# A one-core decoder layer: cached rows are compressed before the first projection instead of beside the state space

## The chip, the cores and the metric

The kernel runs on one core of one Trainium2 chip. The metric is the device time of one execution in microseconds (us), as the median of several runs; lower is better. The profile is of one execution on the same kind of core.

## What is computed

One layer of a decoder, for 512 new tokens of a prompt and for 8 samples of one token each (520 columns in all), in fp32. A conditioning vector gives shift, scale and gate (`mod`) for a normalised input; one projection `w_in` gives the input `u` of a state space model, queries, three pairs of keys and values, and gates. The state space model and an attention with three branches run on their parts; both go through an output projection and then an MLP.

```python
mod = silu(c) @ w_ada + b_ada                     # conditioning, in blocks of 512 columns
h = rmsnorm(x, norm_attn) * (1 + sc1) + sh1
u, q, k_c, v_c, k_s, v_s, k_w, v_w, g = split(h @ w_in)
# state space: B of lambda, u -> scan over time -> C, then
z = gelu(y + d * u);  o_ssm = z * sigmoid(z @ ssm_w_glu)
# compressed branch: cached rows (8 samples x 1024 rows) and new rows
h_first  = einsum('bcjgd,jdh->bcgh', chunks, w1[:16])
h_second = einsum('bcjgd,jdh->bcgh', chunks, w1[16:])
k_cmp = einsum('bngh,hd->bngd', gelu(h_first[:, :-1] + h_second[:, 1:] + pe_term), w2)
```

The change concerns the compressed branch of the samples (the cached rows of each sample, 1 MB, are gathered, turned so that the feature dimension lies on partitions, multiplied by `w1`, put through GELU and multiplied by `w2`), and when this is done.

## The kernel before

Matmuls of projections and MLP are made of three products of rounded halves (wH·xH, wL·xH, wH·xL). The program is written stage by stage; a scheduler then orders the instructions of each engine, so rows of one stage stand among rows of others. Instructions marked `keep_in_program_order` stay in the order in which they are written. Buffers are tiles of named pools: a tile can be written when what read its predecessor in the same place is done, and a pool's memory passes to the next pool when the pool is closed.

The stages, in the order of the program:

- **Constants and loads.** `load_cache(b)` (L246) gathers the 1 MB of sample b on the POOL queue. `late` (L279) issues small loads there.
- **The state space's lambda tables** (L407 to L544), mostly on VectorE: exponentials, sines, tables `tab`, `lr`, `li`.
- **Cache compression, two samples at a time** (bp = 0 to 3). `turned(bp)` (L353) makes 32 transposes of 128x128 on TensorE (`pxc`, L368) into eight PSUM tiles of tag `tr`, which has two buffers, and copies these into two tiles `xc`, one for keys and one for values: four copies a tile, of 64x256, on VectorE (L377) and ScalarE (L375) in turn for bp 0 and 1, all on ScalarE for bp 2 and 3. `compressed(bp)` (L380) multiplies `xc` by `w1` into `ph` (L387: 64 matmuls of some 128 columns for bp 0, 32 of 256 columns for the others), applies GELU (`hidden`, L305) and multiplies by `w2` (`pk`, L396 and L398). An fp32 matmul of this kind is two instructions in the trace.
- **Conditioning** `ada(s)` (L319): 2 MB of `w_ada` in two or four loads (L330), 8 matmuls `pada` (L334), a copy `mrow`, 4 transposes `padt` (L339). s = 0 to 3 are needed before the u projection.
- **u projection** (`pj`, L605), then the first key and value projection `kv_proj(0)` (`pkv`, L647).
- **State space loop** (L727 to L822): 8 groups `qd`. Each makes `BP` and `Cb` (L752 to L759, VectorE), `pm0` and its transposes (L766, L767), sends M to HBM and reads it back as `Tz` (L772, L774, SP queue), makes `pvs` (L792), turns, scans and turns back (`W`, `Rr`, `Sx`, L799 to L811, with ScalarE copies `Vp` and `Rp`), and multiplies `Tz` and `Cb` into `pys` (L819, L820), which goes to HBM as `yscr` (L822). Among the groups stand compressions 2 and 3 with their transposes, `ada` 5 to 9 and `compress_prompt` (L691), which compresses the prompt's own rows with the same `w1`.
- **kv_proj(1), kv_proj(2), q projection** (`pj` again, L900 to L916), whose outputs go to a pool `outs` that takes memory freed by the loop. `state_space_outputs(q)` (L884), for q = 0 to 3, reads `yscr` back as `yc` (L888, one buffer), makes `yf` (L890) and a GELU into `zf`, which is the memory of `uT`.
- **Attention**, among it the scores `psc` (L1159) and `pst` (L1217 to L1219), window rows `rwin`, sums `poS`, and the gate matmuls `pg` (L1273) of the state space, which need all four parts of `zf`; then **out projection** and **MLP** (L1401).

## Time and profile before

| | before |
|---|---|
| median of 3 runs | 896.86 us (896.5 to 897.89) |
| the profiled execution | 896.29 us |
| its span in the trace | 894.6 us |
| TensorE busy (PE) | 844.3 us, 94% |
| VectorE (DVE), ScalarE (ACT), GpSimd (POOL) busy | 525.0, 388.2, 65.2 us |

The span is the time from the first to the last instruction of the trace. Busy times of an engine are sums over its instructions; neighbouring TensorE rows overlap a little. A line such as "L387 PE" is line 387 of the kernel before.

### The profile page before, as it was taken

How to read it: one execution, taken by the hardware profiler on the slowest of the kernel's cores; microseconds unless marked ns; L12 is line 12 of the kernel's file. 1: busy time of each engine (PE TensorE's matmuls, PEld its weight loads, DVE VectorE, ACT ScalarE, POOL GpSimd, SP SyncE). 2: the span in 40 equal slices, each digit the busy share in tenths (PEclk: the TensorE clock that was granted, in tenths of full speed). 3: DMA queues.
4: the chain of work that ended last, by engine and by line, in shares of the span. 5: the costliest groups of instructions: out<-in, count | busy, mean ns of one | idle time of the engine just before them, and what ended most of it. 6: DMA issues, size and time to landing. Idle time of an engine off the chain costs nothing.

```text
span 894.6 us, 16415 instructions
## 1 busy us (share of the span) xinstructions
PE 844.3 (94%) x6517; PEld 747.3 (84%) x6517; DVE 525.0 (59%) x1413; ACT 388.2 (43%) x880; POOL 65.2 (7%) x147
## 2 busy tenths in 40 slices
PE   3799998999999899999889999999999999999995
PEld 2567897788998676756579999999999999999995
DVE  6676656759747975667578964443233444434534
ACT  2545326634435656546655554441111344433422
POOL 6001201000134200100000000000000000000000
PEclk9999999999999999999999999999999999999998
DMA  8956678366456620303257552333333333332202
GB/s 294 318 193 217 194 169 239 123 204 194 127 179 206 203 95 1 142 1 142 78 206 227 161 189 85 95 95 95 95 95 95 95 95 95 96 88 70 79 1 95
DMA packets 111836, 122.36 MB, mean 137 GB/s; under 512 B 24500, under 2 KB 91880, under 8 KB 109584
## 3 DMA queue, kind: packets, MB, share of 16 engines
q1 hardware_dynamic: 102256, 89.71, 33.0%
q0 software_dynamic: 5488, 29.99, 9.8%
q10 hardware_dynamic: 4016, 1.62, 0.7%
q8 instruction: 51, 0.84, 0.4%
q14 instruction: 25, 0.20, 0.1%
HBM read 112.47 MB, written 13.03 MB: 140 GB/s over the span
## 4 chain that ended last, share of the span: by engine, by line
PE 86%; DMA 6%; ACT 3%; DVE 2%; issue 1%; SPq 0%; ACTq 0%; DVEq 0%
PE pdn L1401 21%; PE pup L1401 20%; PE pj L605 5%; PE pwo L1401 5%; PE pkv L647 5%; PE ph L387 5%; DMA wada<-w_ada 5%; PE pada L334 2%; PE ptp L1246 2%; PE po L1253 2%; PE pS L1032 2%; PE pg L1273 2%; PE pst L1217 2%; PE pys L819 2%; PE pkT L1023 1%; PE pst L1218 1%
## 5 line engine op out<-in xcount | busy, mean ns | idle before, releaser
L1401 PE MATMUL pdn<-hidL,wH 128*128 128x256 f32 (+1 forms) x480 | 136.1, 284 | 0.0
L1401 PE MATMUL pdn<-hidH,wL 128*128 128x256 f32 (+1 forms) x480 | 135.9, 283 | 0.0
L1401 PE MATMUL pdn<-hidH,wH 128*128 128x256 f32 (+1 forms) x480 | 135.4, 282 | 0.0
L1401 PE MATMUL pup<-h2L,wH 128*128 128x256 f32 (+1 forms) x480 | 135.0, 282 | 0.0
L1401 PE MATMUL pup<-h2H,wL 128*128 128x256 f32 (+1 forms) x480 | 135.0, 282 | 0.0
L1401 PE MATMUL pup<-h2H,wH 128*128 128x256 f32 (+1 forms) x480 | 134.1, 283 | 0.0
L1401 PEld LDWEIGHTS pup<-h2L,wH 128*128 128x128 f32 x480 | 90.4, 188 | 0.8 <-DVE rs_t L97 0.8
L1401 PEld LDWEIGHTS pdn<-hidH,wL 128*128 128x128 f32 x480 | 90.6, 189 | 0.0
L1401 PEld LDWEIGHTS pdn<-hidL,wH 128*128 128x128 f32 x480 | 90.4, 188 | 0.1
L1401 PEld LDWEIGHTS pup<-h2H,wL 128*128 128x128 f32 x480 | 90.4, 188 | 0.0
L1401 PEld LDWEIGHTS pdn<-hidH,wH 128*128 128x128 f32 x480 | 90.4, 188 | 0.0
L1401 PEld LDWEIGHTS pup<-h2H,wH 128*128 128x128 f32 x480 | 89.6, 188 | 0.0
L63 ACT CAST wH<-wdn 128x1024 fp32r<-128x1024 f32 x30 | 31.5, 1050 | 114.0 <-PE pdn L1401 104.1
L64 DVE TENSOR_TENSOR wL<-wup,wH 128x1024 fp32r<-128x1024 f32 x30 | 36.7, 1224 | 58.1 <-ACT wH L63 58.1
L64 DVE TENSOR_TENSOR wL<-wdn,wH 128x1024 fp32r<-128x1024 f32 x30 | 36.8, 1225 | 54.2 <-ACT wH L63 54.2
L387 PE MATMUL ph<-xc,w 128*128 128x256 f32 (+2 forms) x320 | 65.4, 356 | 1.2 <-DVE xc L377 0.7
L387 PEld LDWEIGHTS ph<-xc,w 128*128 128x128 f32 x320 | 52.8, 203 | 12.9 <-issue 6.4
L63 ACT CAST wH<-wup 128x1024 fp32r<-128x1024 f32 x30 | 31.5, 1050 | 48.0 <-PE pup L1401 37.6
L1479 ACT ACTIVATE rl<-pup 128x256 f32<-128x256 f32 (+1 forms) x64 | 24.4, 384 | 48.9 <-PE pup L1401 48.8
L375 ACT COPY xc<-pxc 64x256 f32<-64x256 f32 x96 | 32.1, 366 | 20.8 <-DVE xc L377 18.2
L1410 DVE SCALAR_TENSOR_TENSOR xT<-pdn,mod,xT 128x256 f32<-128x256 f32 x32 | 15.2, 479 | 43.2 <-PE pdn L1401 43.2
L1480 DVE TENSOR_TENSOR rl<-rl 128x256 f32<-128x256 f32 (+1 forms) x64 | 27.1, 425 | 22.6 <-ACT rl L1479 22.6
(557 smaller groups left out, 2023.9 us busy)
## 6 DMA issues: line engine op xcount, KB each, us to landing
wada<-w_ada SPq DMA_DIRECT2D x20, 1024.0 KB
wup<-w_up SPq DMA_DIRECT2D x16, 1024.0 KB
wdn<-w_down SPq DMA_DIRECT2D x16, 1024.0 KB
wo<-w_out SPq DMA_DIRECT2D x8, 1024.0 KB
wada<-w_ada SPq DMA_DIRECT2D x8, 512.0 KB
rwin<-state_win SPq DMA_DIRECT2D x4, 1024.0 KB
new_win_sample<-state_win POOLq DMA_DIRECT2D x2, 2044.0 KB, 8.9
wkv<-w_in SPq DMA_DIRECT2D x3, 1024.0 KB
```

The source lines that it names most:

```text
L63: nc.scalar.copy(h, src)
L64: nc.vector.tensor_tensor(l, src, h, ALU.subtract)
L334: nc.tensor.matmul(ps[k % 4 * 32 : k % 4 * 32 + 32], cT[:, k], rs[k // kp][:, k % kp], start=(k < 4), stop=(k >= 4))
L375: nc.scalar.copy(dst[:, :, :, hf], srcv[:, :, :, hf])
L387: nc.tensor.matmul(phv[:, lo:hi, 0:w], w1[n][:, r_], xc[n][:, lo:hi, r_ % 8, off : off + w], start=(r_ == 0), stop=(r_ == 15))
L605: nc.tensor.matmul(ps[:, 0:HB], w[:, k], x[:, k, hc], start=(k == 0 and n == 0), stop=(k == KT - 1 and n == 2))
L647: nc.tensor.matmul(ps[0:mp, 0:nw], x[:, k, tok], w[:, k % 4], start=(k == 0 and n == 0), stop=(k == KT - 1 and n == 2))
L819: nc.tensor.matmul(py[:, c], Tz[:, :, :, g].rearrange("p t c -> p (t c)"), U[:, qd * GQ + g], start=True, stop=False)
L1032: nc.tensor.matmul(S[b4 * 32 : b4 * 32 + 32], q4[:, 4 * grp + b4], kts[b4], start=True, stop=True)
L1401: nc.tensor.matmul(ps[:, 0 : b - a], w, x[:, a:b], start=first and n == 0, stop=last and n == 2)
L1479: nc.scalar.activation(rl, ps[:, 0 : b - a], AF.Relu)
L1480: nc.vector.tensor_tensor(rl, rl, rl, ALU.mult)
```

## The change

The compressions of all four sample pairs, and `ada` 0 to 3, are written before the u projection, in the order compressed(0), ada(0), turned(1), compressed(1), ada(1), turned(2), compressed(2), ada(2), turned(3), ada(3), the x transposes, compressed(3). The first conditioning matmul of ada(0) to ada(3) stays in that written order, and ada(1) loads in four parts. The four copies of a PSUM tile in `turned` become two of 64x512, one on VectorE and one on ScalarE, for all bp. The pool with `w1` and `xc` is closed before the u projection and its memory goes to `outs`; `compress_prompt` loads `w1` again (two loads of 1 MB on SP). In the state space loop stand kv_proj(1) after group 0, `compress_prompt` after group 1, kv_proj(2) after group 3, and `ada` 5 to 9 after groups 1, 2, 4, 5 and 6. The q projection has its output memory from the beginning. `state_space_outputs` still takes its memory when the loop's pool is closed.

```diff
@@ loads
     load_cache(2)
-    xr = []
-    for h in range(2):
-        r = p0.tile([P, 2, D], F32, tag="xr%d" % h, name="xr")
...
+    load_cache(3)
...
@@ ada
-    def ada(s, tag, parts=2):
+    def ada(s, tag, parts=2, pin=False):
...
         for k in range(KT):
-            nc.tensor.matmul(ps[k % 4 * 32 : k % 4 * 32 + 32], cT[:, k], rs[k // kp][:, k % kp], start=(k < 4), stop=(k >= 4))
+            mm = nc.tensor.matmul(ps[k % 4 * 32 : k % 4 * 32 + 32], cT[:, k], rs[k // kp][:, k % kp], start=(k < 4), stop=(k >= 4))
+            if pin and k == 0:
+                tc.keep_in_program_order(mm)
@@ turned
-                        for hf in range(2):
-                            if (g + hf) % 2 or bp > 1:
-                                nc.scalar.copy(dst[:, :, :, hf], srcv[:, :, :, hf])
-                            else:
-                                nc.vector.tensor_copy(dst[:, :, :, hf], srcv[:, :, :, hf])
+                        if g:
+                            nc.scalar.copy(dst, srcv)
+                        else:
+                            nc.vector.tensor_copy(dst, srcv)
@@ before the u projection
-    load_cache(3)
-    ada(0, "ad", 4)
-    ada(1, "ad")
+    def two_caches(bp):
+        for b in (2 * bp, 2 * bp + 1):
+            load_cache(b)
+        xcs[bp] = turned(bp)
+
     compressed(0, xcs.pop(0))
-    ada(2, "ad", 4)
+    ada(0, "ad", 4, True)
     xcs[1] = turned(1)
-    ada(3, "ad")
+    compressed(1, xcs.pop(1))
+    ada(1, "ad", 4, True)
+    two_caches(2)
+    compressed(2, xcs.pop(2))
+    ada(2, "ad", 4, True)
+    two_caches(3)
+    ada(3, "ad", 2, True)
...
+    compressed(3, xcs.pop(3))
     p0x.close()
-    compressed(1, xcs.pop(1))
+    cpx.close()
...
+    left = ExitStack()
+    outs = left.enter_context(tc.tile_pool(name="outs", bufs=1, reuse_waits="tile"))
+    QS = outs.tile([P, NH, T], F32R, name="QS")
...
@@ compress_prompt
         for n in range(2):
+            w = rawt("w1p").rearrange("p (r h) -> p r h", r=16)
+            load_w1(n, w)
...
@@ state space loop
-        if qd in (0, 3):
-            b = 4 + 2 * (qd // 3)
-            load_cache(b)
-            load_cache(b + 1)
-            xcs[b // 2] = turned(b // 2)
-        if qd in (2, 5):
-            compressed(2 + qd // 3, xcs.pop(2 + qd // 3))
-        if qd in (1, 3, 4, 6, 7):
-            ada((5, 6, 7, 8, 9)[(1, 3, 4, 6, 7).index(qd)], "ad")
-        if qd == 6:
-            compress_prompt()
...
+        if qd in (0, 3):
+            kv_proj(1 + qd // 3)
+        if qd == 1:
+            compress_prompt()
...
+        if qd in (1, 2, 4, 5, 6):
+            ada((5, 6, 7, 8, 9)[(1, 2, 4, 5, 6).index(qd)], "ad")
@@ behind the loop
-    for c in (1, 2):
-        kv_proj(c)
-        state_space_outputs((c - 1,))
+    state_space_outputs((0,))
     for s in range(2):
...
-        state_space_outputs((2 + s,))
+        state_space_outputs((1,) if s == 0 else (2, 3))
```

The scheduler's order shows what this moves. On TensorE, during compressed(0) (`ph`; w_155 holds the key weights and w_156 the value weights), before:

```order
L334 MATMUL pada<-wada,cT 32x512 x2
L387 MATMUL ph<-xc,w_155 128x128 x3
L334 MATMUL pada<-wada,cT 32x512 x2
L387 MATMUL ph<-xc,w_155 128x128 x6
L435 MATMUL pss<-ones,xsq 8x1 x8
L387 MATMUL ph<-xc,w_155 128x128 x3
L387 MATMUL ph<-xc,w_156 128x130 x3
L334 MATMUL pada<-wada,cT 32x512 x2
L387 MATMUL ph<-xc,w_156 128x130 x13
L339 MATMUL padt<-ident,mrow 128x128 x4
L387 MATMUL ph<-xc,w_156 128x128 x14
L334 MATMUL pada<-wada,cT 32x512
```

and now, the rows that do the same work:

```order
L431 MATMUL pxs<-ident,xsr 128x64
L389 MATMUL ph<-xc,w_155 128x130
L389 MATMUL ph<-xc,w_155 128x128 x15
L437 MATMUL pss<-ones,xsq 8x1 x8
L389 MATMUL ph<-xc,w_155 128x128
L389 MATMUL ph<-xc,w_156 128x130 x16
L389 MATMUL ph<-xc,w_156 128x128 x16
L532 MATMUL pct<-ident,crw 128x128 x4
L538 MATMUL pst_479<-ident,srw 128x128 x2
L557 MATMUL pvec<-ident,vrow 128x84
L371 MATMUL pxc<-ident,rc 128x128 x4
L398 MATMUL pk<-hg,w2k 64x128 x2
```

The conditioning matmuls `pada` that stood between the `ph` rows are gone from there; they come after the transposes `pxc` of turned(1) have begun. Those transposes now follow in one run, with `pada` of ada(0) among them and no `ph`.

On TensorE at the end of the state space loop, before, between the first `pys` matmul of the last group and its others (`psf` are transposes of the final state):

```order
L682 MATMUL pkt<-ident,kvt 128x128 x2
L647 MATMUL pkv<-wH,hH 128x280
L647 MATMUL pkv<-wL,hH 128x280
L647 MATMUL pkv<-wH,hL 128x280
L827 MATMUL psf<-ident,SF 32x128
L647 MATMUL pkv<-wH,hH 128x280
L647 MATMUL pkv<-wL,hH 128x280
L647 MATMUL pkv<-wH,hL 128x280
L647 MATMUL pkv<-wH,hH 128x280
```

and now, from the last `pys` of the seventh group to the first `pys` of the eighth:

```order
L828 MATMUL pys<-Sx,Cb 128x80
L1220 MATMUL pst<-KH,QS 128x512
L1221 MATMUL pst<-KL,QS 128x512
L1222 MATMUL pst<-cmaskr,identr 128x128
L800 MATMUL pvs<-U,Bb 128x72 x4
L1220 MATMUL pst<-KH,QS 128x128
L1221 MATMUL pst<-KL,QS 128x128
L1222 MATMUL pst<-cmaskr,identr 128x128
L1220 MATMUL pst<-KH,QS 128x384
L1221 MATMUL pst<-KL,QS 128x384
L1222 MATMUL pst<-cmaskr,identr 128x128
L827 MATMUL pys<-U,Tz 128x80
```

Rows of key and value projection stood around the last group before; now `pst`, of attention, stands there, and the rows of the q projection are all ahead.

On SP's queue behind the loop, before:

```order
L822 DMA yscr<-ys 128x320
L1263 DMA wglu<-ssm_w_glu 128x4x512
L822 DMA yscr<-ys 128x320
L888 DMA yc<-yscr 16x8x80 x4
L1150 DMA rwin<-state_win 128x2x1024 x3
L888 DMA yc<-yscr 16x8x80 x12
L1150 DMA rwin<-state_win 128x2x1024
```

and now:

```order
L830 DMA yscr<-ys 128x320
L780 DMA mscr<-M_2804 128x64
L782 DMA Tz<-mscr 128x8x64
L830 DMA yscr<-ys 128x320 x2
L893 DMA yc<-yscr 16x8x80 x4
L1153 DMA rwin<-state_win 128x2x1024 x3
L893 DMA yc<-yscr 16x8x80 x4
L1153 DMA rwin<-state_win 128x2x1024
L893 DMA yc<-yscr 16x8x80 x8
```

The reads `yc` still stand behind the last write `yscr`. The eight reads of parts 2 and 3 have moved behind the last `rwin` load; before, that load came last.

## Rows read from the trace of the kernel before

**Rows 1.** The page: busy time by engine, and the chain's shares.

```profile
PE 844.3 (94%) x6517; PEld 747.3 (84%) x6517; DVE 525.0 (59%) x1413; ACT 388.2 (43%) x880; POOL 65.2 (7%) x147
...
PE 86%; DMA 6%; ACT 3%; DVE 2%; issue 1%; SPq 0%; ACTq 0%; DVEq 0%
```

**Rows 2.** Windows: length, busy PE, PEld, DVE, ACT, POOL (instructions), clock, DMA share, GB/s.

```profile
0.00:93.08 93.08, 70.02 (x428) 49.93 (x429) 63.79 (x238) 41.59 (x91) 19.61 (x42) 0.98 0.78 256
133.29:296.38 163.09, 157.98 (x1133) 137.35 (x1131) 115.51 (x300) 80.72 (x216) 32.11 (x79) 1.00 0.59 177
296.38:315.66 19.28, 16.03 (x92) 10.29 (x90) 17.23 (x61) 12.49 (x38) 2.56 (x11) 1.00 0.64 219
```

**Rows 3.** The chain in order of time: start us, us, what.

```profile
15.91 24.38 DMA wada<-w_ada
...
246.35 0.84 PE pvs L792 x8
```

**Rows 4.** Timeline of TensorE, first stretch: start, us, work, [idle before].

```profile
17.57 2.23 PE L368 MATMUL pxc<-ident,rc 128*128 128x128 f32 x8 [3.01 <-DVE xc L377]
...
40.34 1.92 PE L334 MATMUL pada<-wada,cT 128*32 128x512 f32 x4 [2.46 <-DMA wada<-w_ada]
42.19 2.21 PE L387 MATMUL ph<-xc,w 128*128 128x128 f32 x12
...
46.35 1.05 PE L334 MATMUL pada<-wada,cT 128*32 128x512 f32 x4
47.33 3.17 PE L387 MATMUL ph<-xc,w 128*128 128x130 f32 x26
...
58.32 0.71 PE L387 MATMUL ph<-xc,w 128*128 128x128 f32 x4
...
66.27 1.04 PE L368 MATMUL pxc<-ident,rc 128*128 128x128 f32 x8
...
82.00 4.48 PE L387 MATMUL ph<-xc,w 128*128 128x256 f32 x20
...
93.08 0.36 PE L605 MATMUL pj<-hH,wH 128*128 128x260 f32 x1
```

**Rows 5.** Window of 2 us behind a wait, columns as in rows 2.

```profile
40.00:42.00 2.00, 1.66 (x4) 0.19 (x4) 0.00 (x0) 0.00 (x0) 0.00 (x0) 0.52 1.05 388
```

**Rows 6.** Groups of instructions from 133.8 to 297 us: busy, mean ns | idle before.

```profile
L375 ACT COPY xc<-pxc 64x256 f32<-64x256 f32 x64 | 20.3, 366 | 2.2 <-PE pxc L368 1.8
...
L757 DVE TENSOR_TENSOR Cb<-lr,C 128x512 f32<-128x512 f32 x7 | 4.8, 691 | 15.2 <-PE pys L820 15.2
```

**Rows 7.** Timeline of TensorE, state space loop to attention.

```profile
143.02 0.59 PE L819 MATMUL pys<-U,Tz 128*128 128x80 f32 x2
...
256.13 0.34 PE L820 MATMUL pys<-Sx,Cb 128*128 128x80 f32 x2
...
258.15 0.39 PE L820 MATMUL pys<-Sx,Cb 128*128 128x80 f32 x2
...
295.40 1.05 PE L1159 MATMUL psc<-QS,Kcp 128*32 128x512 f32 x4
```

**Rows 8.** Timeline of VectorE.

```profile
55.66 0.75 DVE L531 TENSOR_SCALAR C<-pct,sgn 128x512 f32<-128x512 f32 x1 [1.00 <-PE pct L530]
...
273.38 1.13 DVE L890 SCALAR_TENSOR_TENSOR yf<-uT,vec,yc 128x512 f32<-128x512 f32 x1
...
298.02 1.08 DVE L890 SCALAR_TENSOR_TENSOR yf<-uT,vec,yc 128x512 f32<-128x512 f32 x1
...
310.16 0.69 DVE L113 TENSOR_TENSOR uT<-zt,yf 128x520 f32<-128x520 f32 x1
```

**Rows 9.** Timeline of SP's DMA issues: start, us, issue.

```profile
135.38 0.34 SPq L772 DMA_DIRECT2D mscr<-M  x1
...
138.62 0.37 SPq L774 DMA_DIRECT2D Tz<-mscr  x1
...
259.02 0.32 SPq L822 DMA_DIRECT2D yscr<-ys  x1
```

More of the change, by code (lines that the diff above doesn't have):

```diff
@@ L299, in body @@
         late(srw[:, :, n], i[nm][0].rearrange("(h b) g p -> (b g) h p", h=2))
+    xr = []
+    for h in range(2):
+        r = p0.tile([P, 2, D], F32, tag="xr%d" % h, name="xr")
+        late(r, i["x_prompt"][0, h * 256 : (h + 1) * 256].rearrange("(a p) d -> p a d", p=P))
+        xr += [r[:, 0], r[:, 1]]
     nc.sync.dma_start(w2k[:, 0], i["cmp_w2_k"][0])
@@ L305, in hidden @@
     def hidden(pool, n, ps, w, dst, parts=0, rep=None):
-        x = pool.tile([P, 256], F32, tag="gx", name="gx", bufs=2)[:, 0:w]
-        t1 = pool.tile([P, 256], F32, tag="gt1", name="gt1", bufs=2)[:, 0:w]
+        x = pool.tile([P, w], F32, tag="gx", name="gx", bufs=2)
+        t1 = pool.tile([P, w], F32, tag="gt1", name="gt1", bufs=2)
         if parts:
@@ L593, in body @@
     slx = ExitStack()
-    sl = slx.enter_context(tc.tile_pool(name="sl", bufs=1, reuse_waits="tile"))
+    sl = slx.enter_context(tc.tile_pool(name="sl", bufs=1, side="right", reuse_waits="tile"))
+    left = ExitStack()
+    outs = left.enter_context(tc.tile_pool(name="outs", bufs=1, reuse_waits="tile"))
+    QS = outs.tile([P, NH, T], F32R, name="QS")
+    KH = outs.tile([P, 4, T], F32R, name="KH")
+    KL = outs.tile([P, 4, T], F32R, name="KL")
+    Vx = outs.tile([P, 4, 4, HD], F32, name="Vx")
+    zf = uT
     xTp = sl.tile([P, 2, 2, 8, 32], F32, name="xTp")
@@ L696, in compress_prompt @@
                 off = 0 if r_ < 8 else 1
-                nc.tensor.matmul(ph[:, 0:62], w1[n][:, r_], xTp[:, n, :, r_ % 8, off : off + 31], start=(r_ == 0), stop=(r_ == 15))
+                nc.tensor.matmul(ph[:, 0:62], w[:, r_], xTp[:, n, :, r_ % 8, off : off + 31], start=(r_ == 0), stop=(r_ == 15))
             if n == 0:
-                hg = cp.tile([P, 2, P], F32, tag="hg", name="hgk", bufs=2)[:, 0]
-                hidden(cp, n, ph[:, 0:62], 62, hg[:, 0:62])
+                hg = sl.tile([P, 2, P], F32, tag="hg", name="hgk")[:, 0]
+                hidden(sl, n, ph[:, 0:62], 62, hg[:, 0:62])
                 pk = pst("po", "pkp")
@@ L705, in compress_prompt @@
             else:
-                hv = cp.tile([P, 2, P], F32, tag="hg", name="hgv", bufs=2).rearrange("p g (a n) -> p g a n", a=4)
+                hv = sl.tile([P, 2, P], F32, tag="hg", name="hgv").rearrange("p g (a n) -> p g a n", a=4)
                 nc.gpsimd.memset(hv, 0.0)
-                hidden(cp, n, ph[:, 0:62], 62, hv[:, :, :, 0:31], 0,
+                hidden(sl, n, ph[:, 0:62], 62, hv[:, :, :, 0:31], 0,
                        lambda t: t.rearrange("p (g n) -> p g n", g=2).unsqueeze(2).to_broadcast([P, 2, 4, 31]))
@@ L836, in body @@
     slx.close()
-    cpx.close()
-    left = ExitStack()
-    outs = left.enter_context(tc.tile_pool(name="outs", bufs=1, reuse_waits="tile"))
-    QS = outs.tile([P, NH, T], F32R, name="QS")
-    KH = outs.tile([P, 4, T], F32R, name="KH")
-    KL = outs.tile([P, 4, T], F32R, name="KL")
-    Vx = outs.tile([P, 4, 4, HD], F32, name="Vx")
-    zf = uT
+    srx = ExitStack()
+    gp = srx.enter_context(tc.tile_pool(name="gp", bufs=1, reuse_waits="tile"))
     def add_stats(pool, x, m, key="sq", tmp=("sq", 1)):
@@ L874, in rows_rstd @@
         return rs
-    srx = ExitStack()
     def sraw(name):
         return sr_pool.tile([P, 2048], F32, tag="sraw", name=name, bufs=3)
-    gp = srx.enter_context(tc.tile_pool(name="gp", bufs=1, reuse_waits="tile"))
     def state_space_outputs(qs_):
```

4 lines of the change are left out of this document (1 added, 3 removed).

## The prediction, made before the changed kernel ran

> **What bounds the kernel now.** I read the page first: TensorE is busy 844.3 of 894.6 us, the chain that ended last runs 86% on it, and only 6% of that chain is DMA [rows 1]. So I look for the places where TensorE stands idle or runs slowly, and ask of each moved piece where it lands. The change ends before the out projection, so I then read the windows of the stages before that one. From the start to the first u projection matmul (93.08 us) TensorE is busy 70.02 us; from the end of the first key and value projection to the first attention matmuls (133.29 to 296.38) it is busy 157.98 of 163.09 us [rows 2]. The first stretch is therefore the loose one, and the state space stretch is tight: 5.1 us idle in 163.
>
> The chain shows what holds the first stretch: a load of the conditioning weights, issued at 15.91, lands 24.38 us later [rows 3]. TensorE's rows show the same: it idles 2.46 us before the matmuls at 40.34, and in the early transposes it waits 3.01 us for VectorE's copies [rows 4].
>
> The times below are of one profiled execution, 896.29 us (span 894.6 and 1.7 around it). The median of the three runs shown is 896.86, 0.6 above it.
>
> **The change, part by part.**
>
> *1. Moved work.* Two compressions, with their transposes, leave the state space loop and go ahead of the u projection. Each compression is 32 matmuls (two instructions each), so 128 instructions in all; 20 of them take 4.48 us, which makes 28.7 us. There are 64 transposes; 8 take 1.04 us, which makes 8.3 us [rows 4]. Because neighbouring rows overlap by about a tenth of a microsecond at each change of group, I take 37 us for both.
>
> *2. What the first stretch gives back.* The order now has all 64 matmuls of compressed(0) in one piece, with the conditioning matmuls behind them. Those 128 instructions of 128 columns at 3.17/26 = 0.122 us take 15.6 us; with the last of turned(0)'s tiles copied near 27 (an estimate, 16 longer copies in place of 32) they end near 43.5, since some are done before, against 59.0 (58.32 and 0.71) before [rows 4]. Most of these 15 us go again. The transposes of turned(1) no longer have compressions or conditioning matmuls between them, and each of its eight PSUM tiles is emptied by a VectorE copy and then a ScalarE copy which waits for it. A copy of 64x512 is not in the trace. Below it is bounded by the 64x256 copy at 0.366 us (ScalarE) [rows 6], above by VectorE's 128x512 from PSUM, 0.75 us [rows 8]; I take 0.75, since its columns are the same. Two copies in series with two tiles in flight make about 1.1 us a tile, 1.5 us if nothing overlaps, for 0.52 us of transposes. In turned(1) VectorE has the rest of the lambda preparation between the copies: three products of 128x512 (0.69 us for such [rows 6]), the C copy of 0.75 [rows 8] and many small ones, 8 us by estimate. So compressed(1) can start near 61 (before 69.2). From there: 13.8 us of it, 8 us of turned(2), 14 of compressed(2), 7.5 of turned(3), 20.5 for compressed(3) with the x transposes (4.2) and the last conditioning (2.5) among it: 125, against 93.08 + 37 = 130. That is a gain of 5; it would be 7 with copies that cost nothing more, and a loss of 1 to 3 with 1.5 us a tile.
>
> From this I take off something for the clock. TensorE had been idle for 2.46 us until 40.34; in the window behind it the granted clock is 0.52, the lower of its two levels (1.2 and 2.4 GHz) nearly throughout [rows 5]. Four conditioning instructions took 1.92 us there against 1.05 six microseconds later, and 12 compression instructions 2.21 against 1.46: 1.6 us for one such dip [rows 4]. Early transposes, which wait for copies, also run slowly: 8 take 2.23 us, later 1.04 [rows 4]. Three sparse stretches of transposes stand in the new order. None or three dips are 0 to 5 us; I take 2, since only turned(1) is as sparse as the stretch that ran slowly. **Net: -3 us, bounds -7 and +5.** The Trainium skill (TensorE: Matmul & The Clock Gate, section "HAM oscillation — how this bites in real kernels") says that a wait which recurs between pieces of dense work sends the clock back to half rate each time, and advises to do all dense work of one kind before the next wait; by it all three stretches would pay, 5 us, and the net would be 0. For a full wait rows 5 agree; for a stretch that is only sparse nothing but the early transposes speaks.
>
> The rearranged loads cost nothing: the four early ones land ahead of use, and the two extra 1 MB loads of the compression weights run in the u projection, where TensorE waits for no DMA. Uncovered, one would cost about 5 us.
>
> *3. The state space loop.* Unchanged work shifts by 37 - 3 = 34 us, so the first key and value projection ends near 167.3 (133.3 before [rows 2]). The rest until attention was 162.1 us (133.3 to 295.40) and loses 37 of work: 125, so 292.4, if TensorE stays as full. The loop by itself needs 9.7 us to its first output matmuls (143.02) and 115.5 from there to its last (258.54): 167.3 + 125.2 = 292.5 [rows 7]. The two limits meet, so there is no slack: key and value and q projections now fill exactly what the loop leaves. Before, 37 us of them came behind the loop and covered the last group's tail.
>
> That is the first new wait. In the new order no projection row is left when the eighth group comes: between the seventh group's last output matmul and the eighth's stand three small sets of attention score matmuls (about 1.9 us by the same sets from 296.38 on) and the state transposes. From the last group's pvs (246.35) to its second output matmul 9.8 us pass [rows 3, 7], in which VectorE and ScalarE rotate, scan and rotate back; 0.8 of it is pvs itself. Exposed, this is at most 7 us, at least 2 if VectorE is free at once; I take 5. The scores done there are saved later, so +3.1 (0 to +5).
>
> VectorE's load: 115.5 of 163 us [rows 2], less about 6.5 of the four moved GELUs and 12.4 of three outputs that go to attention: 96.6 in 125 by my sums of its rows, or 77% against 71%. It is no bound, but already now its Cb multiply waits 15.2 us in all for the output matmuls of the group before [rows 6], so its work comes in bursts. I take +1, bounds -2 and +8 (seven steps at 17.6 us for 16.5).
>
> *4. The state space outputs.* Before, the loop ended 37 us ahead of attention, and three of the four reads, yf and GELU ran beside the q projection; the fourth ended with uT at 310.16, 5 us before the gate matmuls, which begin where the last window ends, at 315.66 [rows 2, 8]. Now all four follow the last group (near 297.5). yscr is written 0.5 us after [rows 9]; such a write and the read behind it take 3.2 us (from M's issue to Tz's, 135.38 to 138.62 [rows 9]) and about 4 more to land: first yf near 305. Three steps at 8.2 us (273.38 to 298.02 [rows 8]), or 6.6 if only the chain counts, put the last yf at 325 to 330 and its end at 332 to 336. The order has moved the gate matmuls behind other attention work, and in pieces: by the rows of before, TensorE comes to the last piece near 330. It waits 2 to 6 us, less what other waits of that stretch cover (between 296.38 and 315.66 TensorE is busy 16.03 us, so 3.3 are idle already [rows 2]): +2.5, bounds 0 and +8.
>
> **Sum.** -3 + 3.1 + 1 + 2.5 = +3.6: 896.3 + 3.6 = 899.9, so 900. Later stages keep their times.
>
> **The rivals.** (a) *Faster.* The state space chain stays hidden. TensorE's waits for conditioning loads go (-7), the loop with fewer rows of other work in its way keeps 16.5 us or less, and the gate matmuls find zf ready: -7 + 2 = 891, or 887 with 0.5 us less a step. It needs the early stretch to end before 124. For it speak that 15 us come free by 43.5 and that 20.3 us of ScalarE copies [rows 6] leave the loop; against it that the loop and TensorE's work meet at 292.5. (b) *No change.* Early gain and last tail cancel at 895 to 898.6: -4, 3 and 1. (c) *The transposes decide*, slower: 1.5 us a tile and a slow clock in three stretches, +5 early, and the later terms on top: 905 to 912. For it speak the slow early transposes; against it that turned(2) and turned(3) find VectorE almost free. The page on the clock gate named above would favour it.
>
> **How the numbers follow.** A difference under 0.2% (1.8 us) can't be told from none here. My forecast (899 to 905) gets 0.34, (c) 0.16, (b) 0.17, (a) 0.33. So slower 0.50, same 0.17, faster 0.33. The range runs from the low end of (a), less 1, to the high end of (c): 886 to 912; the forecast's own is 897 to 905.
>
> **What would show it.** In the profile of the changed kernel: compressed(0) ends near 44 with no idle before conditioning matmuls; the copies of 64x512 take about 0.75 us; u projection starts near 127 (122 or less: (a); 133 or more: (c)); the granted clock in 44 to 61 is under 1; the last output matmul is near 297, with TensorE idle some 5 us ahead of it; and an idle time at the gate matmuls is put down to uT. I am wrong if ScalarE and VectorE copies overlap better than two tiles let me think, if the loop steps are clearly shorter than 16.5 us, or if attention, waiting on exponentials anyway, hides the late outputs.

## The result, and the profile after

The changed kernel takes 955.22 us (median of 4 runs, 953.39 to 961.49) against 897.08 (896.5 to 897.89): 1.0656 times as long, interval 1.0621 to 1.0691. The forecast was 900 with a range of 886 to 912, so the time lies 43 us above the range. The profiled execution took 953.39 us, with a span of 951.7.

The page of the changed kernel: busy time by engine, the granted clock of TensorE in 40 equal slices (tenths of the full clock; 9 is 90% or more), and the chain's shares.

```profile
PE 861.4 (91%) x6517; PEld 761.4 (80%) x6517; DVE 547.2 (57%) x1413; ACT 391.0 (41%) x816; POOL 68.9 (7%) x147
...
PEclk9978999999979868999999999999999999999998
...
PE 77%; DVE 9%; ACT 6%; DMA 5%; issue 1%; SPq 1%; POOL 0%; ACTq 0%; DVEq 0%; POOLq 0%
```

TensorE issues the same 6517 instructions as in [rows 1], but is busy 17.1 us longer, and it is idle 90.3 us instead of 50.3. The two add up to the 57.1 us by which the span grew. The clock row has two dips (a slice is 23.8 us): one in slices 3 and 4, from 48 to 95 us, and one in slices 12 to 16, from 262 to 381 us (with one 9 among them). And VectorE and ScalarE hold 15% of the chain instead of 5%.

To see where the time went, I cut the span at two events that both kernels have: the first key and value matmul (`pkv`, 118.20 before and 173.00 now) and the first matmul of the out projection (`pwo`, 449.80 and 503.50). Inside, the first and last `pys` bound the state space loop. The windows of the changed kernel (length, busy PE, PEld, DVE, ACT, POOL, clock, DMA share, GB/s):

```profile
0.00:144.60 144.60, 108.45 (x632) 83.24 (x633) 90.38 (x262) 66.03 (x99) 23.58 (x47) 0.93 0.59 192
...
173.00:503.50 330.50, 293.95 (x2089) 226.00 (x2088) 222.82 (x627) 154.32 (x403) 42.60 (x94) 0.93 0.47 143
197.40:324.60 127.20, 117.93 (x853) 105.09 (x852) 90.37 (x235) 50.93 (x134) 18.56 (x47) 0.93 0.53 165
324.60:503.50 178.90, 152.64 (x1043) 98.55 (x1042) 115.46 (x343) 96.15 (x255) 24.04 (x48) 0.92 0.37 127
```

And of the kernel before, in the same order from the second on:

```profile
118.20:449.80 331.60, 316.46 (x2297) 246.06 (x2296) 227.59 (x647) 176.50 (x475) 41.38 (x97) 1.00 0.46 141
143.00:258.30 115.30, 114.12 (x803) 101.10 (x802) 83.02 (x224) 52.09 (x140) 11.57 (x37) 1.00 0.55 172
258.30:449.80 191.50, 180.07 (x1309) 125.60 (x1308) 128.89 (x374) 113.54 (x306) 28.28 (x60) 1.00 0.35 117
```

This is the whole case in three numbers. Ahead of `pkv`: +54.8 us, which are the 37 us of moved work and 17.8 more; of these, 14.5 stand ahead of the first u projection matmul (`pj`, 144.60 for 93.08 [rows 4]) and 3.3 in the u projection. From `pkv` to `pwo`: 330.5 against 331.6, so 208 TensorE instructions left this stretch and it became 1.1 us shorter. From `pwo` to the end: +3.4 us (448.2 for 444.8). In the middle stretch TensorE's busy time fell by 22.5 us and its idle time rose by 21.4 (15.1 to 36.6), while the clock went from 1.00 to 0.93.

TensorE's timeline ahead of the u projection, changed kernel (start, us, work, idle before), answers to [rows 4]:

```profile
26.90 4.13 PE L389 MATMUL ph<-xc,w 128*128 128x130 f32 x24
...
44.72 0.60 PE L371 MATMUL pxc<-ident,rc 128*128 128x128 f32 x4
...
51.08 1.12 PE L371 MATMUL pxc<-ident,rc 128*128 128x128 f32 x4 [2.74 <-ACT xc L377]
53.26 1.12 PE L371 MATMUL pxc<-ident,rc 128*128 128x128 f32 x4 [1.07 <-ACT xc L377]
...
64.90 13.98 PE L389 MATMUL ph<-xc,w 128*128 128x256 f32 x64
78.72 0.38 PE L371 MATMUL pxc<-ident,rc 128*128 128x128 f32 x2
...
94.03 13.98 PE L389 MATMUL ph<-xc,w 128*128 128x256 f32 x64
107.85 0.38 PE L371 MATMUL pxc<-ident,rc 128*128 128x128 f32 x2
...
122.19 3.62 PE L389 MATMUL ph<-xc,w 128*128 128x256 f32 x16
...
144.60 0.39 PE L624 MATMUL pj<-hH,wH 128*128 128x260 f32 x1
```

compressed(0) ends where the forecast put it, near 44, and a compression takes 13.98 us as forecast (13.8). The transposes are what is late: turned(2) lasts 15.3 us (78.72 to 94.03) and turned(3) 14.3 (107.85 to 122.19), where 8 and 7.5 were forecast. The groups of the changed kernel's first 145 us say why (busy, mean ns of one, idle before):

```profile
L377 ACT COPY xc<-pxc 64x512 f32<-64x512 f32 x32 | 33.2, 1037 | 22.5 <-DVE xc L379 21.8
L379 DVE COPY xc<-pxc 64x512 f32<-64x512 f32 x32 | 33.1, 1033 | 11.3 <-PE pxc L371 10.5
...
L371 PE MATMUL pxc<-ident,rc 128*128 128x128 f32 x128 | 25.1, 336 | 23.5 <-ACT xc L377 21.5 <-DVE vec L558 2.0
```

A copy takes 1.03 us, not 0.75. ScalarE waits for VectorE's copy and TensorE for ScalarE's: 21.5 us in this stretch.

### The profile page after: what moved, and what is told of

The parts are those of the page before. It is cut to its first block, busy times and chain, and to the rows that moved or that the text cites. A ratio compares the mean times of both kernels' runs of the same rounds, so it can differ in the third digit from the quotient of the medians.

```text
span 951.7 us, 16335 instructions
## 1 busy us (share of the span) xinstructions
PE 861.4 (91%) x6517; PEld 761.4 (80%) x6517; DVE 547.2 (57%) x1413; ACT 391.0 (41%) x816; POOL 68.9 (7%) x147
## 4 chain that ended last, share of the span: by engine, by line
PE 77%; DVE 9%; ACT 6%; DMA 5%; issue 1%; SPq 1%; POOL 0%; ACTq 0%; DVEq 0%; POOLq 0%
PE pdn L1404 19%; PE pup L1404 19%; PE pj L624 5%; PE pwo L1404 5%; PE ph L389 4%; PE pkv L666 3%; PE pada L335 2%; DMA rwin<-state_win 2%; PE po L1256 2%; PE ptp L1249 2%; DVE xc L379 2%; PE pg L1276 2%; PE pys L827 1%; PE pS L1035 1%; ACT xc L377 1%; PE pxc L371 1%
## 5 line engine op out<-in xcount | busy, mean ns | idle before, releaser
L1404 PEld LDWEIGHTS pup<-h2L,wH 128*128 128x128 f32 x480 | 90.3, 188 | 2.6 <-issue 1.7
L389 PE MATMUL ph<-xc,w 128*128 128x256 f32 (+2 forms) x320 | 59.1, 343 | 0.0
L371 PE MATMUL pxc<-ident,rc 128*128 128x128 f32 x128 | 25.1, 336 | 23.5 <-ACT xc L377 21.5
L371 PEld LDWEIGHTS pxc<-ident,rc 128*128 128x128 f32 x128 | 17.3, 169 | 33.5 <-ACT xc L377 27.8
L1482 ACT ACTIVATE rl<-pup 128x256 f32<-128x256 f32 (+1 forms) x64 | 24.4, 383 | 44.9 <-PE pup L1404 44.8
L377 ACT COPY xc<-pxc 64x512 f32<-64x512 f32 x32 | 33.2, 1037 | 22.5 <-DVE xc L379 21.8
```

What stands on the lines that cost most here:

```text
L371: nc.tensor.transpose(ps[:, jp * P : (jp + 1) * P], rv[:, 2 * jp + j2, n], ident)
L377: nc.scalar.copy(dst, srcv)
L389: nc.tensor.matmul(phv[:, lo:hi, 0:w], w1[n][:, r_], xc[n][:, lo:hi, r_ % 8, off : off + w], start=(r_ == 0), stop=(r_ == 15))
L1404: nc.tensor.matmul(ps[:, 0 : b - a], w, x[:, a:b], start=first and n == 0, stop=last and n == 2)
L1482: nc.scalar.activation(rl, ps[:, 0 : b - a], AF.Relu)
```

## The experiments

The table has every kernel that ran. Columns: median; ratio to the kernel before on the same chip, with its interval; then, of the profiled execution, the start of the first `pkv`, the loop (first to last `pys`), the time from there to the first `pwo`, the whole from `pkv` to `pwo`, and the clock in that whole.

| kernel | us | ratio | `pkv` at | loop | behind | `pkv` to `pwo` | clock |
|---|---|---|---|---|---|---|---|
| before | 897.08 | | 118.2 | 115.3 | 191.5 | 331.6 | 1.00 |
| changed | 955.22 | 1.066 [1.062, 1.069] | 173.0 | 127.2 | 178.9 | 330.5 | 0.93 |
| e1_split | 946.72 | 1.057 [1.048, 1.066] | 163.5 | 124.5 | 181.4 | 331.4 | 0.94 |
| e2_order | 939.53 | 1.046 [1.039, 1.054] | 160.4 | 126.2 | 177.8 | 330.2 | 0.93 |
| e3_shift_late | 949.06 | 1.055 [1.048, 1.063] | 172.8 | 127.0 | 178.3 | 329.5 | 0.92 |
| e4_kv2_behind | 944.65 | 1.053 [1.046, 1.059] | 172.8 | 121.7 | 175.7 | 322.5 | 0.95 |
| e5_before_merged | 931.52 | 1.038 [1.034, 1.041] | 125.3 | 130.6 | 196.5 | 356.7 | 0.95 |
| e6_before_order | 929.34 | 1.036 [1.032, 1.040] | 124.3 | 127.6 | 199.9 | 353.1 | 0.96 |
| e7_kv_behind | 953.02 | 1.062 [1.059, 1.066] | 172.2 | 116.9 | 178.1 | 328.1 | 0.92 |
| e8_three | 942.81 | 1.052 [1.048, 1.056] | 158.8 | 121.8 | 181.9 | 329.1 | 0.94 |
| e9_swap | 904.88 | 1.010 [1.007, 1.013] | 118.3 | 115.3 | 194.2 | 334.2 | 0.98 |
| e10_loads | 902.01 | 1.007 [1.003, 1.011] | 121.6 | 114.9 | 191.4 | 332.1 | 0.99 |
| e11_after_swap | 945.09 | 1.055 [1.051, 1.058] | 159.3 | 128.4 | 185.1 | 338.5 | 0.92 |
| e12_more_vector | 908.88 | 1.013 [1.009, 1.016] | 116.7 | 121.0 | 189.9 | 337.1 | 0.99 |
| e13_less_pe | 941.79 | 1.051 [1.044, 1.057] | 173.8 | 107.9 | 185.1 | 322.4 | 0.89 |
| e14_no_low | 958.60 | 1.069 [1.064, 1.074] | 172.9 | 112.6 | 193.2 | 333.7 | 0.91 |
| e15_before_q1 | 910.20 | 1.014 [1.011, 1.017] | 117.7 | 117.3 | 197.7 | 340.4 | 0.94 |
| e16_q_behind | 959.32 | 1.069 [1.065, 1.073] | 173.7 | 124.3 | 184.3 | 335.1 | 0.90 |
| e17_q_behind_order | 942.46 | 1.051 [1.046, 1.056] | 157.9 | 123.8 | 184.7 | 334.0 | 0.91 |
| e18_q_behind_rwin | 950.69 | 1.058 [1.052, 1.065] | 159.1 | 124.1 | 193.6 | 343.8 | 0.90 |

**The copies.** e1_split keeps the change and goes back to four copies of 64x256 a tile.

```diff
-                        if g:
-                            nc.scalar.copy(dst, srcv)
-                        else:
-                            nc.vector.tensor_copy(dst, srcv)
+                        for hf in range(2):
+                            if (g + hf) % 2 or bp > 1:
+                                nc.scalar.copy(dst[:, :, :, hf], srcv[:, :, :, hf])
+                            else:
+                                nc.vector.tensor_copy(dst[:, :, :, hf], srcv[:, :, :, hf])
```

> The changed kernel with the four copies of 64x256 per transposed tile that it had before (VectorE and ScalarE in turn for the first two pairs of samples, ScalarE alone for the others). My theory now: about 21 us of the loss lie ahead of the u projection, and most of them in the merged copies, which take 1.04 us each and stand in series on two engines, 2.1 us a tile. With four copies a tile should take 1.5 to 1.6 us, so each of the four stretches of transposes loses 3 to 4 us and the u projection starts near 139 instead of 151.5: 940 to 945 us. Rival: the stretches are long because nothing else stands among the transposes and VectorE has the lambda work; then the copies' form changes 0 to 4 us: 951 or more.

The first `pj` starts at 137.2 instead of 144.60 (the 151.5 of the expectation is where its rows go on after a wait), so 7.4 us come back ahead of it and not 12.5; the time, 946.72, lies between the two forecasts.

e2_order keeps the two merged copies and only writes their 512 elements in another order: 64 columns innermost in place of the pair `hf`, whose members lie 2,112 bytes apart in `xc`. Every engine's order of instructions is that of the changed kernel.

```diff
-dst = dst.rearrange("p (hf jp) c -> p jp c hf", hf=2)
-srcv = ps[...].rearrange("p (jp c hf) -> p jp c hf", jp=4, hf=2)
+dst = dst.rearrange("p (hf jp) c -> p hf jp c", hf=2)
+srcv = ps[...].rearrange("p (jp c hf) -> p hf jp c", jp=4, hf=2)
```

> The changed kernel with the merged copies' inner dimension changed: 64 columns inside, halves outside, instead of two halves inside. The same 512 elements a partition and the same two instructions a tile. If the innermost pair, which scatters over distant places of the tile, is what makes a copy take 1.04 us, it falls to 0.65 to 0.75 us and the time to 938 to 945 us. If 512 elements of 64 partitions out of PSUM simply cost 1.04 us, nothing changes: 951 to 957.

The two groups in e2_order:

```profile
L379 DVE COPY xc<-pxc 64x512 f32<-64x512 f32 x32 | 21.8, 682 | 6.2 <-PE pxc L371 5.2
L377 ACT COPY xc<-pxc 64x512 f32<-64x512 f32 x32 | 18.6, 580 | 20.6 <-DVE xc L379 20.1
```

So the innermost pair costs 0.35 us on VectorE and 0.46 on ScalarE for the same elements. Without it the first `pj` starts at 130.4, 14.2 us earlier. That brings `pkv` forward by 12.6 us of the 17.8, and the time by 15.7. The Trainium skill (SBUF — State Buffer, section "Door 1: The DMA port swizzle (why `[64,N]` ≈ `[32,N]`)") says that accesses which stay in a 16-byte line run at full speed and each new line costs; these two rows agree, since the pair changes line with every element. On the reading side it is the other way round: in PSUM the members of a pair are neighbours, and with the columns innermost the read takes every second element.

e5_before_merged puts the merged copies of the change into the kernel before, alone; e6_before_order does so with e2_order's inner order.

```diff
-for hf in range(2):
-    if (g + hf) % 2 or bp > 1: ...
+if g:
+    nc.scalar.copy(dst, srcv)
+else:
+    nc.vector.tensor_copy(dst, srcv)
```

> The kernel before with one part of the change alone: the four copies of a transposed tile become two of 64x512, innermost pair inside, one on VectorE and one on ScalarE. Copies of 1.04 us make a tile 2.1 us in series instead of 1.6, and VectorE gets 16 of them in the state space loop that it had not. If the copies' form by itself is a loss wherever it stands: 902 to 910. If it hurts only where nothing else stands among the transposes (before, compressions and conditioning do): 896 to 900.

> The kernel before with merged copies whose inner dimension is the 64 columns (0.68 us on VectorE, 0.58 on ScalarE as measured in the changed kernel). A tile takes 1.3 us instead of 1.6 and ScalarE's load falls: 892 to 897 if the early transposes lie on the path, no change if they do not.

Both forecasts missed by more than 20 us. Here half of these copies stand in the loop, and the stretch from `pkv` to `pwo` grows by 25.1 and 21.5 us. VectorE's busy time in it grows by 15 and 10, since it now takes a copy of each tile of turned(2) and turned(3), all of which ScalarE made before. The parts don't add up: this edit alone costs 35 us in the kernel before, and without it (e1) the change still costs 49.

**The scatter of orders.** e9_swap exchanges VectorE and ScalarE for the copies of turned(0) and turned(1) in the kernel before, and e11_after_swap does so for all copies in e2_order; neither adds work, but the scheduler makes another order. e10_loads has the change's order of the early loads alone.

```diff
# e9_swap
-if (g + hf) % 2 or bp > 1:
+if (g + hf) % 2 == 0 or bp > 1:
# e11_after_swap
-if g:
+if not g:
# e10_loads: load_cache(3) to the early loads, both loads of xr from there behind srw's
```

> The kernel before with one edit that changes no work: of the four copies of a transposed tile in the first two pairs of samples, the two that VectorE did go to ScalarE and the other way round. The scheduler makes another order of it (a quarter of TensorE's rows stand elsewhere). If the order of the kernel before is an unusually good one, and most other orders leave TensorE idle a little more and its clock low now and then, this takes 905 to 930, as both runs with merged copies did. If it was the merged copies that cost 30 us there, this takes 893 to 900.

> The changed kernel with 64 columns inside in the merged copies, VectorE and ScalarE exchanged: the same work and another order. Against 939.5 for the same without the exchange. If orders scatter by chance, this lies anywhere in 925 to 955; if the structure sets the time, 937 to 942.

> The kernel before with the change's new order of the early loads alone (the fourth gather early, the prompt's rows behind the small loads). By its work it should be 892 to 898. If any new order costs, 905 to 930.

An edit that adds nothing costs 7.8 us on the kernel before and 5.6 on e2_order. Differences below about 8 us between kernels of different order can't be put down to an edit here by time alone. e10_loads moves `pkv` by 3.4 us, which e9_swap doesn't (0.1). A part of the scatter stands behind the change: from `pwo` to the end six kernels take 443.6 to 444.9 us (before, e3, e4, e10, e11, e13) and the fourteen others 448.1 to 449.8, e9 with no changed work among them (448.4). In e9 and in the changed kernel a matmul `pup` of the MLP waits 2.1 us there, in the kernel before none does; the changed kernel's wait:

```profile
PE pup L1404 <- ACT h2H L200: 2.1, 1, 2.1
```

**What stands behind the loop.** In the changed kernel TensorE's waits from the last `pys` to `pwo` are headed by the window loads (us in total, times, longest):

```profile
PE pkT L1026 <- DMA rwin<-state_win: 9.2, 2, 7.5
PE ptp L1249 <- DVE pe L1235: 3.7, 4, 1.8
```

e3_shift_late moves the work on these loads back in attention's list, e4_kv2_behind writes the third key and value projection behind the loop, e7_kv_behind the second too. e8_three has the edits of e2, e3 and e4 together.

```diff
# e3_shift_late
-        win_shift(grp)
+        12: [sample_out, lambda: win_shift(0), lambda: win_shift(1)],
# e4_kv2_behind
-        if qd in (0, 3):
-            kv_proj(1 + qd // 3)
+        if qd == 0:
+            kv_proj(1)
+    kv_proj(2)          # behind state_space_outputs((0,))
# e7_kv_behind: neither in the loop, and behind it as before
+    for c in (1, 2):
+        kv_proj(c)
+        state_space_outputs((c - 1,))
```

> The changed kernel with the two 2 MB copies of the window state to the output issued late in attention instead of just ahead of the window rows' loads. Theory: TensorE waits for the window rows behind the loop (7.5 us in one piece, with 9 us idle and a low clock in 23 us) because they share the DMA engines with these copies; without them the last needed row lands by 340 instead of 348 and the time falls by 6 to 10 us, to 944 to 949. Rival: the loads are late because their memory comes free only when the loop ends, and they take as long by themselves: within 2 us of 955.

> The changed kernel with the third key and value projection written behind the state space loop, as before the change. Theory: nothing covers the last group's tail, the window rows and the state space outputs, so 15 us of projection behind the loop cover 10 to 20 us of what TensorE now stands idle or runs slowly: 935 to 945. Rival: the projection only moves, and the loop, with less beside it, stands idle itself: 952 to 958.

> The changed kernel with both the second and the third key and value projection behind the state space loop, as before the change, and the state space outputs among them as before. If the loop is held by its own chain (VectorE, the two transfers of M, ScalarE), it stays 115 to 127 us long with 30 us less work beside it, TensorE idles there and the gain of moving the third projection is given back: 945 to 960. If the loop is held by TensorE's rows, it shrinks by 10 to 15 us more and the time falls below that of the run with the third projection alone behind it: 928 to 940.

> Three edits of the changed kernel together: copies with 64 columns inside, the copies of the window state late, the third key and value projection behind the loop. By themselves they gave about 16, 6 and 10 us against the changed kernel's 955. If they act at different places: 922 to 926. If the late window rows and the uncovered end of the loop are one loss: 927 to 934. What is left above 897 lies then in the clock and in idle of the stretches of transposes and of attention.

In e3_shift_late the wait for `rwin` falls to 1.0 us, and the stretch behind the loop stays (178.3): the wait was a place where the lost time showed, not its cause. The time falls by 6.2 us all the same, but 4.5 of it stand behind `pwo` (443.7 for 448.2), which the edit doesn't touch. The scheduler undid most of e4 and e7. In e4 not one projection matmul stands behind the last `pys`; all 386 of the loop are in it as in the changed kernel, in another order, and that order is 8.0 us shorter from `pkv` to `pwo`, no more than the scatter; that 944.65 lies within the forecast is luck. In e7 27 rows of q got behind the loop, and 48 of `pkv` from ahead of it into it; the loop is 10.3 us shorter, and 8.7 are lost again ahead of it (33.1 us from `pkv` to the first `pys`, 24.4 in the changed kernel). So these two don't test what they were made for; e16_q_behind, below, does. e8_three missed its forecast of 922 to 934: it takes 942.81, 3.3 more than e2 alone, so the gains of its three edits don't add up.

**One engine at a time.** Over the first eleven runs the loop's length followed VectorE's busy time in it (115.3 us with 83.0, up to 130.6 with 95.8). Four kernels tested that. e12_more_vector issues one product three times; e13_less_pe leaves two of three products out of q and the later keys and values; e14_no_low leaves out the subtractions for the weights' low part and multiplies by the high part twice; e15_before_q1 leaves two of three products out of q in the kernel before.

```diff
# e12_more_vector (kernel before)
+for _ in range(3):
     nc.vector.tensor_tensor(tmp, lam_b(li, 1), vec_b(C1p[:, gs]), ALU.mult)
# e13_less_pe; e15_before_q1 has the last pair of lines only
-for n, (x, w) in enumerate(((hH, wh), (hH, wl), (hL, wh))):
+for n, (x, w) in enumerate(((hH, wh), (hH, wl), (hL, wh))[:n3]):   # n3 = 1 for c > 0
-for hf, ps in proj_half(wh, wl):
+for hf, ps in proj_half(wh, wl, 1):
# e14_no_low
-split(h, l, r)
+nc.scalar.copy(h, r)        # and h is used for l
```

> The kernel before, with one more kind of work on VectorE alone: in each of the eight steps of the state space loop the product tmp = li times C1p (128x512, 0.69 us) is written three times instead of once, so 16 x 0.69 = 11 us more of VectorE between the first and the last pys, and not one instruction more on TensorE. Nothing is left out. Theory 1 (VectorE's work sets the loop's length): the loop goes from 115.5 to 125 to 130 us, the time to 906 to 912. Rival (TensorE's work and its waits for copies set it, VectorE has slack): loop 115.5 to 119, time 897 to 901.

> The changed kernel, with TensorE's work in the loop cut and VectorE's kept: of the three products of the q projection and of the second and third key and value projection only the first is computed (two of three are left out, so q, k and v lose their low parts): 128 + 160 matmuls fewer, at 0.122 us some 35 us, of which about 258 matmuls or 31 us stood between the first and the last pys. Theory 1 (VectorE sets the loop): the loop stays 122 to 128 us and the whole falls only by the rows ahead of the loop and a little more, to 944 to 953. Rival (TensorE's work sets the loop): the loop falls from 127.6 to about 97 to 105, the time to 922 to 930.

> The changed kernel, with VectorE's work in the loop cut and TensorE's kept: the subtraction that makes the low half of the weights of q and of the second and third key and value projection is left out (six of 128x1024 at 1.22 us and two small ones, 7.8 us of VectorE, about 7.2 of them in the loop), and the high half stands in its place in the matmuls, so these projections lose the weights' low part. Theory 1 (VectorE sets the loop): loop 127.6 to 117 to 121, time 944 to 949. Rival (TensorE's work sets it): loop 125 to 128, time 952 to 957.

> The kernel before, with two of the three products of the q projection left out: 128 matmuls at 0.122 us, 15.6 us less of TensorE behind the state space loop, nothing else. Theory 2 (the projections behind the loop cover the reading back of the state space, the selection on VectorE and the window loads, so that work taken away from there is given back as waits): from the last pys to the first pwo 191.3 becomes 182 to 188, the time 888 to 893. Rival (no cover: TensorE is the bound there): 191.3 becomes 175 to 177, the time 881 to 883.

Windows from `pkv` to `pwo` and of the loop, e12_more_vector:

```profile
116.70:453.80 337.10, 318.28 (x2298) 246.72 (x2296) 236.94 (x667) 177.88 (x475) 40.58 (x97) 0.99 0.47 146
142.90:263.90 121.00, 120.34 (x845) 106.58 (x844) 88.54 (x236) 53.40 (x145) 8.71 (x31) 0.99 0.52 163
```

e13_less_pe:

```profile
173.80:496.20 322.40, 271.82 (x1800) 199.34 (x1800) 223.53 (x627) 154.35 (x403) 38.61 (x94) 0.89 0.47 147
203.20:311.10 107.90, 88.22 (x568) 74.14 (x566) 87.53 (x230) 47.83 (x125) 13.69 (x45) 0.83 0.57 184
```

e14_no_low, the whole and the loop:

```profile
172.90:506.60 333.70, 295.73 (x2088) 226.17 (x2087) 215.75 (x617) 153.98 (x403) 37.45 (x94) 0.91 0.46 142
200.80:313.40 112.60, 106.94 (x831) 96.70 (x830) 81.56 (x221) 49.28 (x129) 12.88 (x45) 0.98 0.56 177
```

e15_before_q1, the whole and the part behind the loop:

```profile
117.70:458.10 340.40, 315.74 (x2168) 239.83 (x2168) 227.94 (x651) 176.34 (x475) 42.63 (x97) 0.94 0.47 145
260.40:458.10 197.70, 176.27 (x1181) 116.92 (x1180) 129.21 (x378) 113.60 (x306) 29.61 (x60) 0.92 0.37 127
```

The theory that VectorE alone sets the loop falls. Less TensorE work shortens the loop by 19.3 us (e13), though VectorE's busy time in it falls by 2.8 only; less VectorE work shortens it by 14.6 (e14). e12 doesn't decide: its loop grows by 5.7 us, not by 10 to 15, but only 5.5 of the 11 us of VectorE show in it, and the new order put 42 more TensorE instructions (6.2 us) into it, so either theory would give that. But from `pkv` to `pwo` almost nothing of that arrives. e13 has 289 instructions fewer there than the changed kernel (288 by the edit), 35 us at the full clock, and is 8.1 us shorter. e14 gives all of its 14.6 back behind the loop (193.2 for 178.9). e15 has 129 instructions fewer than the kernel before (128 by the edit) and is 8.8 us longer, with TensorE busy just as long (315.74 for 316.46) at a clock of 0.94 instead of 1.00; its rows wait 4.4 us for ScalarE's copies of q, where the kernel before waits 1.4. Both theories stated for e15 expected a gain.

**The projection put back.** e16_q_behind holds the q projection behind the loop of the changed kernel, e17_q_behind_order does the same to e2_order, and e18_q_behind_rwin adds the window loads in other buffers.

```diff
# e16, and in e2_order e17
-nc.tensor.matmul(ps[:, 0:HB], w[:, k], x[:, k, hc], ...)
+mm = nc.tensor.matmul(ps[:, 0:HB], w[:, k], x[:, k, hc], ...)
+if pin and k == 0 and n == 0:
+    tc.keep_in_program_order(mm)
# e18: e17 and
-r = sraw("rwin").rearrange("p (b f) -> p b f", b=2)
+r = rawt("rwin").rearrange("p (b f) -> p b f", b=2)
```

> The changed kernel, with the first matmul of each half of the q projection held behind the state space loop's code, so that all 192 rows of it stand behind the seventh group's last output matmul (18 of them still ahead of the eighth's), where the order before had them. Theory 2 (dense projection rows behind the loop cover waits there and keep the clock up): the loop falls from 127.2 to 108 to 116 us, and the stretch from the last pys to the first pwo grows by much less than the 23 us that the rows take, from 178.9 to 183 to 192; with what the earlier stages keep, 938 to 948 us. Rival (the rows are worth their own length wherever they stand): the loop falls by 10 to 15, the stretch grows to 200 to 204, the time stays 953 to 960.

> The same as e16_q_behind with the copies of e2_order (the 64 columns innermost), and so e2_order with the q projection held behind the loop. Theory 2: e2_order's 939.5 less the gain of e16_q_behind, 922 to 932 us, with the granted clock of the 60 us behind the last pys above 0.9. Rival: 937 to 944.

> e17_q_behind_order with the four window loads in the three buffers of the weights in place of those that take the memory of the state space loop, so the first need not wait for the loop's end. If the window loads' wait, and not the lack of dense rows, is what lengthens the stretch behind the loop, this is 5 to 10 us faster than e17_q_behind_order; if dense rows are there to cover it, it is within 4 us of it.

The first 80 us behind the last `pys`, changed kernel, where the q projection stands ahead of them:

```profile
324.60:404.60 80.00, 63.45 (x394) 40.63 (x394) 52.13 (x161) 35.90 (x92) 20.26 (x44) 0.84 0.50 164
```

and e16_q_behind, the same 80 us and then its loop:

```profile
324.50:404.50 80.00, 75.43 (x513) 53.67 (x511) 58.54 (x171) 48.29 (x130) 18.64 (x48) 1.00 0.45 150
...
200.20:324.50 124.30, 105.18 (x671) 89.74 (x669) 79.64 (x208) 37.23 (x95) 13.40 (x41) 0.78 0.51 157
```

and the kernel before, with its q rows in the same place:

```profile
258.30:338.30 80.00, 75.20 (x529) 58.25 (x528) 59.12 (x170) 46.58 (x127) 22.60 (x54) 1.00 0.51 168
```

Behind the loop the theory of cover held. With q's rows there the clock is 1.00 instead of 0.84, TensorE is busy 12 us more of the 80, the window loads are waited for no more, and the stretch grows by 5.4 us where the 174 rows that came behind the last `pys` would take 21 alone (at 0.122 us). In the loop it failed: with 182 matmuls fewer the loop is 2.9 us shorter. Its clock is 0.78, and TensorE now waits there for the state space's own steps (waits in e16_q_behind's loop):

```profile
PE pys L830 <- POOL Sx L823: 5.0, 2, 4.5
PE pys L829 <- DMA Tz<-mscr: 4.2, 3, 1.7
PE psf L845 <- DVE SF L822: 2.9, 1, 2.9
```

So the whole gains nothing: 959.32 us lies in the range of the rival. e17 repeats that on e2_order (loop 123.8 for 126.2, whole +3.8; 942.46, again the rival's). e18 is 8 us slower than e17, which neither theory expected, and settles nothing: e17 no longer waits for the window loads, so there was no wait to save, and e18 waits in new places (6.9 us for ScalarE's copies of q, 3.5 for the load `rslc`).

## Why the prediction was wrong

**The moved work** was right: 37 us, with 13.98 us a compression, and compressed(0) ended at 44.

**"Net: -3 us, bounds -7 and +5" for the first stretch**, up to the first `pj`, measured +14.5. The step that failed is "I take 0.75, since its columns are the same": a row of the same size in another order of elements was used as an upper bound. It was 1.03, two in a row for each tile, and the sentence on copies that run one behind the other was right (21.8 us of ScalarE's wait). With the other inner order 14.2 of the 14.5 us go away. The 0.3 left stand against -3 to -5 by the forecast's own terms with such copies, so 3 to 5 us of this stretch have no run that explains them. "The rearranged loads cost nothing", because TensorE waits for no DMA in the u projection, failed as well. In the changed kernel it waits there for a conditioning load:

```profile
150.42 1.07 PE L335 MATMUL pada<-wada,cT 128*32 128x512 f32 x8 [2.14 <-DMA wada<-w_ada]
```

e10_loads, the new order of the loads alone, waits 2.2 us in the same place and has `pkv` 3.4 us later; the kernel before doesn't wait there. In the changed kernel the u projection takes 3.3 us longer than before.

**"The rest until attention ... loses 37 us of work: 125, so 292.4, if TensorE stays as full"** is the step that cost most. By the sum, the stretch from `pkv` to `pwo` would have been 331.6 - 37 + 6.6 = 301.2; it was 330.5, so 29.3 of the 53.5 us by which the span (951.7) missed the forecast's (898.2); 20.8 of the others stand ahead of `pkv` and 3.4 behind `pwo`. I had read 1.00 in the clock column and 158 busy us of 163 as a limit set by TensorE. The rows of work that I moved were also what kept TensorE full while the state space's steps, and later attention's exponentials and window loads, were on their way. Taken away they left their places as waits and as a lower clock: without the 37 us TensorE's busy time would have been some 279.5 us (an estimate, 316.5 - 37) and was 294.0, so 14.5 us are rows that took longer, and 21.4 more us are idle. e13, e15 and e16 agree from three sides: matmuls taken out of this stretch bring 8.1 of 35 us and -8.8 of 15.6, and matmuls moved inside it from loop to attention restore the clock there (1.00 for 0.84) and lower the loop's (0.78 for 0.93).

**The loop's +1 ("It is no bound")** became +11.9. It isn't VectorE alone, as e13 and e16 showed; that it is the loop's chain over both engines fits the runs, but no run shows it by itself. **The last group's tail** (5 us exposed, bounds 2 and 7; +3.1 with the score matmuls saved) was right in kind and within its bounds, by TensorE's timeline of the changed kernel:

```profile
318.15 0.67 PE L827 MATMUL pys<-U,Tz 128*128 128x80 f32 x2 [0.79 <-DMA Tz<-mscr]
...
321.53 0.40 PE L843 MATMUL psf<-ident,SF 128*32 128x128 f32 x1 [2.49 <-DVE SF L820]
```

These are 3.3 us of waits; no projection rows are left there. **The gate matmuls (+2.5)** don't wait for `uT` in the changed kernel, where the window loads are waited for first; in e3, with those mostly gone, they wait 0.9 us for it. **"Later stages keep their times"** missed 3.4 us, which e9, with no changed work, shows as well (3.6).

On the clock, the forecast took one dip of 1.6 us from [rows 5] and allowed three of them. The changed kernel has a clock of 0.93 over 330 us. The Trainium skill (TensorE: Matmul & The Clock Gate, section "HAM oscillation — how this bites in real kernels") says that short pieces of dense work with waits for loads between them pay for the clock each time; the 80 us at 0.84 against 1.00 with q's rows in them agree. I had weighed this rule only for the transposes.

**What stays open.** What sets the some 330 us is not settled. No run had less TensorE work there and a clock of 1.00, so which of the two, the lower clock or the waits for the chain of state space and attention, brings on the other wasn't told apart. Nor did a run put independent rows back into the changed kernel's stretch. A new order by itself remains a rival: each of these edits made one, and e5 and e6 lose 25.1 and 21.5 us in this stretch with all of TensorE's rows in place. e4 (322.5), whose rows only changed places in the loop, may be a better order or scatter. None of the kernels beats the one before.

## What to carry to other kernels

A stretch in which TensorE is busy 97% at full clock isn't thereby bound by TensorE. If a serial chain of other engines runs under it, the independent matmuls may be its cover; moved out here, they cost their full 37 us at the new place and brought 1.1 us at the old one. Before moving work out, estimate from the chain that remains how long the stretch takes with that work gone altogether; a kernel that just leaves it out measures that. Price a merged copy by a row with the same innermost run, not only the same size.

## What the runs showed that I had not expected

- A PSUM to SBUF copy of 64x512 with pairs innermost takes 1.03 us on VectorE and 1.04 on ScalarE; with 64 columns innermost 0.68 and 0.58.
- 128 matmuls fewer made a kernel 12 us slower (e15, ratio 1.014; 3.5 of it behind `pwo`), with TensorE's busy time from `pkv` to `pwo` nearly unchanged (315.7 for 316.5 us).
- Exchanging two engines' equal halves of the copies costs 6 to 8 us through the scheduler's order alone.
- Loops with the same steps ran at clocks of 1.00 (115.3 us), 0.93 (127.2) and 0.78 (124.3, 182 matmuls fewer).
